# A SwiGLU feed-forward with seven-product duos: the last difference of the up product is written into its PSUM bank, and one plain weight tile waits for the duo's end

## The chip, the cores and the metric

The kernel runs on one core of a Trainium2 chip. The metric is the device time of one launch in microseconds (us). The engines are named as in the profile: PE (TensorE, matmuls), PEld (its weight loads), DVE (VectorE), ACT (ScalarE), POOL (GpSimd) and SP (SyncE, which here issues the weight loads from HBM).

## The reference

Two layers over 256 tokens of width 2048, in float32: gated linear attention, then a SwiGLU feed-forward; then shared keys and values, differential attention over them, and a second SwiGLU feed-forward. The change is in the feed-forward:

```python
def swiglu(h, w_gate_up, w_down):
    gate, up = jnp.split(h @ w_gate_up, 2, axis=-1)
    return (jax.nn.silu(gate) * up) @ w_down
...
        f = swiglu(rmsnorm(x, pre_ffn_g[i]), ffn_w_gate_up[i], ffn_w_down[i])
        x = x + rmsnorm(f, post_ffn_g[i])
```

`w_gate_up` is 2048 x 11264 and `w_down` 5632 x 2048.

## The kernel before

**Tiles.** Tokens are two blocks of 128. Weights are read once, in tiles of 128 x 1024 float32: two neighbouring 128-row pieces of the contraction, 512 columns each. SP loads a tile into one of five `raw` buffers; ACT casts it to a high part `hi` (L298); DVE subtracts to get the low part `lo` (L301). High and low parts lie in nine slots until PE is done with them. Each product of a 128 x 128 activation piece with a 128 x 512 weight piece takes three matmuls (high by high, high by low, low by high): `triple` (L484 to 488) in the duos, `mm_act` (L402 to 413) elsewhere.

**Duos.** The 5632 gate columns are 11 chunks of 512, the up columns 11 more. Chunk 0 is multiplied plainly. Each of chunks 1 to 10 is a duo: gate chunk c and up chunk 11 + c together, for both token blocks, over eight steps s of the contraction. A plain step costs eight products (24 matmuls, two weight tiles: w1 of the gate, w2 of the up). A fast step (0, 2, 3, 4, 5, 6; for chunk 1 only 0, 2, 4, 6) takes seven products (21 matmuls) on sums and differences, in Strassen's manner. Its weight tiles are called a, b, c and d: DVE forms the sums in place (four operations at L333), a, b and c are converted as tiles of 1024 columns, d as one of 512. The prepared activation sums are `f_ffn_fast` and `f_ffn_rest`; `h_ffn` holds the plain activations.

**Banks.** The products of a duo go to eight PSUM banks called `ps[0]` to `ps[7]`: 0 to 5 from a pool of six (`acc` in the profile), 6 and 7 from a pool of two (`tp`), which the transposes use as well. When the last fast step is done, `early` combines banks 0, 4, 5 and 6. Plain steps add the gate's products to banks 1 and 3 (one per token block), the up's to 2 and 7; when the last plain step has finished a bank, `late` adds it to what `early` left. For the gate, ACT then takes the Silu (L1208); for the up part, `gated` (L1190) multiplies it by the gate. The result `sg` is transposed on PE (L655) for the down product (`gate_T`).

**Order.** The tile framework puts each engine's work in an order of its own from the order in which it is issued. `weight_stream` fixes the order of the weight tiles and so of SP's loads. `take` converts ahead as far as the buffers allow. `behind(n)` issues its work behind the conversion of the nth tile ahead, so its number says how many conversions stand before an operation in DVE's queue; `urgent` lets an operation go to the front of what is ready; `defer(n, ...)` issues work n ticks of the matmul loops later. Between duos, the down product adds to banks that ACT has filled from `f_ffn` (L464) and that ACT copies back (L1261).

Of the kernel before, what the change touches and what calls it, by code (L numbers as in the profile page):

```python
# [15 lines left out]
ALU = mybir.AluOpType  # L16
AX = mybir.AxisListType

P = 128
D = 2048  # L20
SEQ = 256
KT = D // P
C = 512
# [21 lines left out]
SKEW, LAST_SKEW = 7, 8  # L45
CHAIN = (3, 4, 5, 6)
FIRST_X = {1: [(1, 0), (0, 1)], 3: [(1, 1)], 5: [(0, 2)], 7: [(1, 2)], 9: [(0, 3)], 11: [(1, 3)]}
NRAW, NRING = 5, 9
EARLY_BEHIND, LATE_BEHIND, DOWN_BEHIND, GATE_BEHIND = 3, 3, 0, 0
NEW_SUMS = ('w_g',)  # L50
V_BEGIN, V_EVERY, V_Q = 16, 3, 1

# [1 line left out]
def ffn_pairs(c):  # L54

    return FAST_SECOND if c == 1 else FAST_FFN
# [26 lines left out]
def weight_stream():  # L83

    out = []

    def chunk(name, n, ns=8, s0=0):
        out.extend((name, (n, s0 + s), "plain") for s in range(ns))

    def block(name, n):  # L90
        out.extend((name, (n, s), "plain") for s in range(2))

    def duo(c1, c2, fast):
        for s in range(8):
            if s in fast:
                out.extend(("duo", (c1, c2, s), kind) for kind in ("a", "b", "c", "d"))
            else:
                out.extend((name, (n, s), "plain") for name, n in (c1, c2))

    def ffn(i):  # L100
        for kind, which, *chunks in ffn_steps():
            if kind == "down":
                out.extend((f"w_d{i}", (c, 2 * which[0] + s), "plain") for c, s in down_order(which, *chunks))
            elif which == 0:
                chunk(f"w_gu{i}", 0)
                chunk(f"w_gu{i}", 11)
# [12 lines left out]

    def middle_duo(name, fast):  # L120
        chunk(name, 0)
        duo((name, 1), (name, 2), fast)
        chunk(name, 3)

    middle_duo("gla_w_out", FAST_OUT)
    ffn(0)
    chunk("w_v", 0)
    chunk("w_v", 3)
    duo(("w_v", 1), ("w_v", 2), FAST_V)
    for name in ("w_k", "diff_w_q"):  # L130
        for n in range(KT):
            block(name, n)
    middle_duo("diff_w_out", FAST_OUT)
    ffn(1)
    return out

# [52 lines left out]
class Trunk:  # L189
# [142 lines left out]
    def add(self, out, in0, in1):  # L332
        return self.nc.vector.tensor_tensor(out=out, in0=in0, in1=in1, op=ALU.add)  # L333
# [145 lines left out]
            for u in range(n, len(order)):  # L479
                run(u, b)  # L480

    def triple(self, ps, a, w, j, first, last):
        nc = self.nc
        ah, al = a  # L484
        wh, wl = (t[:, j * C : (j + 1) * C] for t in w)
        nc.tensor.matmul(ps, ah, wh, start=first, stop=False)  # L486
        nc.tensor.matmul(ps, ah, wl, start=False, stop=False)  # L487
        nc.tensor.matmul(ps, al, wh, start=False, stop=last)  # L488

    def duo_act(self, aT, forms, fast, c1, c2, early, late):  # L490

# [688 lines left out]
    def gated_duo(self, hT, forms, w, c, rs, new_sg):  # L1180

        nc = self.nc
        made = []

        def op(out, in0, in1, how):
            nc.vector.tensor_tensor(out=out, in0=in0, in1=in1, op=how)

        def gated(b, up):
            sg = made[0]
            nc.vector.scalar_tensor_tensor(  # L1190
                out=sg[:, b, :], in0=up, scalar=rs[b], in1=sg[:, b, :], op0=ALU.mult, op1=ALU.mult
            )

        def early(ps):
            made.extend((new_sg(), self.scratch(), self.scratch()))
            sg, v, y = made
            nc.scalar.copy(sg[:, 0, :], ps[0])
            op(v, ps[5], sg[:, 0, :], ALU.subtract)
            op(sg[:, 1, :], ps[6], v, ALU.subtract)
            op(y, ps[4], sg[:, 1, :], ALU.subtract)  # L1200
            op(v, ps[4], v, ALU.add)

        def late(bank, ps):
            sg, v, y = made
            if bank in (1, 3):
                b = bank // 2
                op(sg[:, b, :], ps[bank], sg[:, b, :], ALU.add)
                nc.scalar.activation(sg[:, b, :], sg[:, b, :], AF.Silu, scale=rs[b])  # L1208
            else:
                b, part = (0, v) if bank == 2 else (1, y)  # L1210
                op(part, ps[bank], part, ALU.add)
                gated(b, part)

        self.duo_apart(hT, forms, ffn_pairs(c), ((w, c), (w, 11 + c)), early, late)
        return made[0]

    def ffn(self, fp, hT, rs, gi, wgu, wd, post, after, name, reload, side=None):
        nc = self.nc
        self.narrow, self.n_narrow = (fp, 2, 2), 0
        forms = Forms(FAST_FFN, range(8), self.whole(4, [P, 4, 2, 4, P], f"{name}_fast", F32R))  # L1220
# [7 lines left out]
        first, last = FF_GROUPS[0], FF_GROUPS[-1]  # L1228
# [42 lines left out]
        f = []  # L1271
        plan = ffn_steps()
        for n, (kind, which, *chunks) in enumerate(plan):
            if kind == "up":
                sg = self.gated_duo(hT, forms, wgu, which, rs, new_sg) if which else gated_first()
                follow = plan[n + 1]
                wait = 4
                if follow[0] == "down" and which not in follow[1]:
                    wait = 2 * len(down_order(*follow[1:])) + 1
                self.defer(wait, lambda sg=sg, c=which: gate_T(sg, c))  # L1280
                continue
            chunks, skew = chunks[0], 0
            if not f:
                f.append(self.whole(5, [P, 2, D], name))
                if side:
                    self.defer(5, side)
            if which == last:
                if chunks[0] == 0:
                    reload()
                else:  # L1290
                    skew = LAST_SKEW
                for c in chunks:
                    gains[c] = self.gain(post, c)

# [158 lines left out]
    def run(self):  # L1453
        nc, tc, t = self.nc, self.tc, self.t
        self.setup()
        self.pool_lo.update((3, 5))
        hT = self.pair(0, "h_mix0")
        rs = []

        def reload(src, name):  # L1460
            self.x = self.whole(4, [P, 2, D], name)
            for b in range(2):
                nc.sync.dma_start(self.x[:, b, :], src[b])

        with tc.tile_pool(name="gla", bufs=1) as gp:
            oT = self.gla(gp, hT, rs)
            rs = []
            x_mix0 = self.dram.tile([2, P, D], F32, tag="x_mix0", name="x_mix0")
            hT = Split([])
# [179 lines left out]
```

## Time and profile before

| what | value |
|---|---|
| median of three runs | 2168.73 us (2167.71 to 2168.75) |
| profiled execution | 2168.14 us, its span 2166.4 us |
| PE busy in the span | 2151.2 us (99%) |
| DVE busy | 1953.3 us (90%) |
| ACT busy | 1374.2 us (63%) |
| the duos of the first feed-forward | about 430 to 1045 us of the span |
| the duos of the second | about 1510 to 2123 us of the span |

In the rows of the profile `acc<-lo,h_ffn` means output from inputs, with the buffers' numbers left out; "x4" counts instructions, and a bracket at the end says how long the engine had been idle before and what released it. A matmul's shown duration overlaps the next one's, so the distance between starts tells PE's speed. DVE's operations overlap a little in the same way.

### The profile page before, as it was taken

The numbers are of one execution on the slowest core, as the hardware profiler recorded it, in microseconds if no ns is written. First come the engines' busy times: TensorE is split into PE (matmuls) and PEld (weight loads), VectorE is DVE, ScalarE is ACT, GpSimd is POOL, SyncE is SP. The second block draws the span as 40 slices with busy tenths as digits, with TensorE's granted clock in tenths as the row PEclk, the third lists the DMA queues.
The fourth block names the chain that finished last, engine by engine and source line by source line (L and its number), as shares of the span: only waits on it lengthen the run. The fifth ranks groups of instructions, "written<-read, shape, count | busy, mean of one in ns | idle before, by whom it ended". The sixth has DMA issues, their size and how long they took to land.

```text
span 2166.4 us, 28415 instructions
## 1 busy us (share of the span) xinstructions
PE 2151.2 (99%) x10044; PEld 1787.7 (83%) x10044; DVE 1953.3 (90%) x2686; ACT 1374.2 (63%) x1926; POOL 37.1 (2%) x66
## 2 busy tenths in 40 slices
PE   9999999999999999999999999999999999999998
PEld 8888788888888888888778888888888888888886
DVE  7989988999999999999798567889999999999996
ACT  8756655666666666666776445556656666666664
POOL 1000000000000000000000000000000000000000
PEclk9999999999999999999999999999999999999999
DMA  8546566666565666656767655465665566665664
GB/s 310 166 150 192 174 226 219 219 199 227 173 209 203 211 211 195 223 190 211 254 200 245 185 179 159 155 226 202 225 195 187 177 207 214 212 209 201 203 225 155
DMA packets 123317, 440.10 MB, mean 203 GB/s; under 512 B 13900, under 2 KB 16629, under 8 KB 121381
## 3 DMA queue, kind: packets, MB, share of 16 engines
q1 hardware_dynamic: 121996, 436.44, 60.4%
q10 hardware_dynamic: 1176, 1.84, 0.2%
q8 instruction: 79, 1.29, 0.2%
q14 instruction: 66, 0.53, 0.1%
HBM read 429.82 MB, written 9.97 MB: 203 GB/s over the span
## 4 chain that ended last, share of the span: by engine, by line
PE 93%; DVE 4%; issue 1%; ACT 1%; DMA 1%; SPq 0%; POOL 0%; DVEq 0%; POOLq 0%; ACTq 0%
PE acc L488 12%; PE acc L487 12%; PE acc L486 12%; PE acc L413 11%; PE acc L412 11%; PE acc L411 11%; PE acc L634 8%; PE acc L635 4%; PE tp L487 2%; PE tp L486 2%; PE tp L488 2%; DVE lo L301 2%; PE tp L655 1%; DVE raw L333 1%; DMA raw<-in_w_d_dram 1%
## 5 line engine op out<-in xcount | busy, mean ns | idle before, releaser
L301 DVE TENSOR_TENSOR lo<-raw,hi 128x1024 fp32r<-128x1024 f32 x921 | 1096.2, 1220 | 115.1 <-ACT hi L298 108.8
L298 ACT CAST hi<-raw 128x1024 fp32r<-128x1024 f32 x923 | 943.9, 1051 | 356.5 <-DVE raw L333 91.5
L412 PE MATMUL acc<-lo,f_ffn_gT 128*128 128x512 f32 x704 | 273.5, 389 | 0.1
L411 PE MATMUL acc<-hi,f_ffn_gT 128*128 128x512 f32 x704 | 270.4, 389 | 0.0
L413 PE MATMUL acc<-hi,f_ffn_gT 128*128 128x512 f32 x704 | 269.0, 389 | 0.0
L487 PE MATMUL acc<-lo,h_ffn 128*128 128x512 f32 x612 | 238.7, 390 | 0.0
L488 PE MATMUL acc<-hi,h_ffn 128*128 128x512 f32 x612 | 238.4, 389 | 0.0
L486 PE MATMUL acc<-hi,h_ffn 128*128 128x512 f32 x612 | 227.8, 390 | 0.0
L333 DVE TENSOR_TENSOR raw<-raw 128x512 f32<-128x512 f32 x232 | 159.5, 687 | 3.4
L411 PEld LDWEIGHTS acc<-hi,f_ffn_gT 128*128 128x128 f32 x704 | 132.2, 188 | 28.4 <-issue 0.6
L412 PEld LDWEIGHTS acc<-lo,f_ffn_gT 128*128 128x128 f32 x704 | 132.1, 188 | 27.9 <-DVE lo L301 0.6
L413 PEld LDWEIGHTS acc<-hi,f_ffn_gT 128*128 128x128 f32 x704 | 132.2, 188 | 27.4
L486 PEld LDWEIGHTS acc<-hi,h_ffn 128*128 128x128 f32 x612 | 114.9, 188 | 24.2 <-ACT hi L298 0.4
L488 PEld LDWEIGHTS acc<-hi,h_ffn 128*128 128x128 f32 x612 | 114.9, 188 | 23.5
L487 PEld LDWEIGHTS acc<-lo,h_ffn 128*128 128x128 f32 x612 | 114.9, 188 | 23.5
L298 ACT CAST hi<-sum 128x512 fp32r<-128x512 f32 x72 | 44.8, 622 | 101.1 <-DVE sum L333 101.1
L634 PE MATMUL acc<-h_q,hi 128*128 128x512 f32 x256 | 92.5, 401 | 0.0
L634 PE MATMUL acc<-h_kv,hi 128*128 128x512 f32 x256 | 90.7, 399 | 0.0
L634 PE MATMUL acc<-h_mix,hi 128*128 128x512 f32 x256 | 90.6, 398 | 0.0
L1261 ACT COPY f_ffn<-acc 128x512 f32<-128x512 f32 x80 | 45.8, 586 | 66.4 <-PE acc L413 66.4
L298 ACT CAST f_ffn_rest<-sum 128x512 fp32r<-128x512 f32 x56 | 34.9, 623 | 80.9 <-DVE sum L333 80.9
L333 DVE TENSOR_TENSOR sum<-raw,raw 128x512 f32<-128x512 f32 x116 | 79.4, 685 | 0.0
(415 smaller groups left out, 4128.6 us busy)
## 6 DMA issues: line engine op xcount, KB each, us to landing
raw<-in_w_gu_dram SPq DMA_DIRECT2D x352, 512.0 KB, 4.5
raw<-in_w_d_dram SPq DMA_DIRECT2D x176, 512.0 KB, 4.8
raw<-in_gla_w_r_dram SPq DMA_DIRECT2D x32, 512.0 KB, 4.8
raw<-in_gla_w_v_dram SPq DMA_DIRECT2D x32, 512.0 KB, 4.1
raw<-in_gla_w_out_dram SPq DMA_DIRECT2D x32, 512.0 KB, 4.5
raw<-in_w_v_dram SPq DMA_DIRECT2D x32, 512.0 KB, 4.4
raw<-in_w_k_dram SPq DMA_DIRECT2D x32, 512.0 KB, 4.4
raw<-in_diff_w_q_dram SPq DMA_DIRECT2D x32, 512.0 KB, 3.5
```

The costliest lines, as they stand in the source:

```text
L298: cast = nc.scalar.copy(hi, src)
L301: rest = eng.tensor_tensor(out=lo, in0=src, in1=hi.bitcast(F32), op=ALU.subtract)
L333: return self.nc.vector.tensor_tensor(out=out, in0=in0, in1=in1, op=ALU.add)
L411: nc.tensor.matmul(ps, ah, rh, start=(kt == 0 and not onto), stop=False, skip_group_check=onto)
L412: nc.tensor.matmul(ps, ah, rl, start=False, stop=False, skip_group_check=onto)
L413: nc.tensor.matmul(ps, al, rh, start=False, stop=(kt == 2 * ns - 1), skip_group_check=onto)
L486: nc.tensor.matmul(ps, ah, wh, start=first, stop=False)
L487: nc.tensor.matmul(ps, ah, wl, start=False, stop=False)
L488: nc.tensor.matmul(ps, al, wh, start=False, stop=last)
L634: nc.tensor.matmul(ps, lh, aT.both(kt), start=(kt == 0), stop=False)
L635: nc.tensor.matmul(ps[:, SEQ:], ll, aT.hi(kt), start=False, stop=(kt == KT - 1))
L1261: nc.scalar.copy(fc, ps)
```

## The change

`gated_duo` uses a new function, `duo_seeded`, in place of `duo_apart`.

- `early` writes the difference that it used to keep in scratch `y` straight into bank 7, before any matmul of that bank. All matmuls of bank 7 then add onto it (none starts the bank afresh).
- `late` of bank 7 no longer adds bank and scratch; `gated` reads the bank itself.
- Where a step other than 7 is plain (step 1; for chunk 1 steps 1, 3 and 5), its w1 tile stays in place, and its w2 tile is held back to step 7: the stream there is kept w2, w1 of step 7, w2 of step 7. Kept w2 goes to bank 2 at once and to bank 7 after banks 1 and 3 are finished.
- Banks 2 and 6 now come from the pool `tp`; 0, 1, 3, 4, 5 and 7 from `acc`.
- `early` is issued urgent, and EARLY_BEHIND falls from 3 to 1. The gate transposes of chunk 0 are deferred by 1 tick instead of 4.
- `reload_by_parts` and its two constants are added and not called.

```diff
-EARLY_BEHIND, LATE_BEHIND, DOWN_BEHIND, GATE_BEHIND = 3, 3, 0, 0
+EARLY_BEHIND, LATE_BEHIND, DOWN_BEHIND, GATE_BEHIND = 1, 3, 0, 0
...
     def duo(c1, c2, fast):
+        apart = c1[0][:4] == "w_gu"
+        kept = [s for s in range(7) if s not in fast] if apart else []
         for s in range(8):
+            if s == 7:
+                out.extend((c2[0], (c2[1], s), "plain") for s in kept)
+            if s in kept:
+                out.append((c1[0], (c1[1], s), "plain"))
+                continue
...
+    def duo_seeded(self, aT, forms, fast, chunks, early, late):
...
+                ps[bank] = self.tp().rearrange("p j t -> p (j t)") if bank in (2, 6) else self.acc()
...
+            if last:
+                bank_of(7)
+                with self.behind(EARLY_BEHIND):
+                    self.urgent(early)(ps)
+        kept = [(s, self.take(w2, (n2, s))) for s in held]
+        for s, wp in kept:
+            plain(2, s, 0, wp, False)
+        wp = self.take(w1, (n1, 7))
+        for b, bank in enumerate((1, 3)):
+            plain(bank, 7, b, wp, True)
+        for s, wp2 in kept:
+            plain(7, s, 1, wp2, False, True)
+            self.free()
+        self.free()
+        wp = self.take(w2, (n2, 7))
+        plain(2, 7, 0, wp, True)
+        plain(7, 7, 1, wp, True, True)
+        self.free()
...
-            made.extend((new_sg(), self.scratch(), self.scratch()))
-            sg, v, y = made
+            made.extend((new_sg(), self.scratch()))
+            sg, v = made
...
-            op(y, ps[4], sg[:, 1, :], ALU.subtract)
+            op(ps[7], ps[4], sg[:, 1, :], ALU.subtract)
...
-            else:
-                b, part = (0, v) if bank == 2 else (1, y)
-                op(part, ps[bank], part, ALU.add)
-                gated(b, part)
-
-        self.duo_apart(hT, forms, ffn_pairs(c), ((w, c), (w, 11 + c)), early, late)
+            elif bank == 2:
+                op(v, ps[bank], v, ALU.add)
+                gated(0, v)
+            else:
+                gated(1, ps[bank])
+
+        self.duo_seeded(hT, forms, ffn_pairs(c), ((w, c), (w, 11 + c)), early, late)
...
-                wait = 4
+                wait = 4 if which else 1
```

The order of work changes in the duos of both feed-forward stages. DVE at the end of chunk 5's duo in the first stage, before. `hs` and `sg` are the scratch and the gate buffer, `lo` rows are conversions, and the first L1186 row reads `ps[5]`:

```order
L301 TENSOR_TENSOR lo_1233_6434<-raw_1214_6347,hi_1232_6433 128x1024
L301 TENSOR_TENSOR lo_1236_6446<-raw_1205_6297,hi_1235_6445 128x1024
L301 TENSOR_TENSOR lo_1239_6463<-raw_1217_6359,hi_1238_6462 128x1024
L301 TENSOR_TENSOR lo_1242_6475<-raw_1225_6393,hi_1241_6474 128x1024
L301 TENSOR_TENSOR lo_1245_6487<-raw_1228_6405,hi_1244_6486 128x1024
L1186 TENSOR_TENSOR hs_1266_6559<-acc_1196_6270,sg_1265_6558 128x512
L301 TENSOR_TENSOR lo_1248_6499<-raw_1234_6437,hi_1247_6498 128x1024
L1186 TENSOR_TENSOR sg_1265_6558<-tp_1192_6258,hs_1266_6559 128x512
```

The same place on DVE now. `lo_1231` is the held-back tile, `lo_1234` the gate's tile of step 7, and `acc_1257` is bank 7:

```order
L309 TENSOR_TENSOR lo_1225_6407<-raw_1206_6320,hi_1224_6406 128x1024
L309 TENSOR_TENSOR lo_1228_6419<-raw_1197_6279,hi_1227_6418 128x1024
L309 TENSOR_TENSOR lo_1231_6436<-raw_1209_6332,hi_1230_6435 128x1024
L1259 TENSOR_TENSOR hs_1259_6533<-acc_1193_6267,sg_1258_6532 128x512
L309 TENSOR_TENSOR lo_1234_6448<-raw_1217_6366,hi_1233_6447 128x1024
L1259 TENSOR_TENSOR sg_1258_6532<-tp_1187_6248,hs_1259_6533 128x512
L309 TENSOR_TENSOR lo_1237_6460<-raw_1220_6378,hi_1236_6459 128x1024
L309 TENSOR_TENSOR lo_1240_6472<-raw_1226_6410,hi_1239_6471 128x1024
L1259 TENSOR_TENSOR acc_1257_6531<-acc_1198_6281,sg_1258_6532 128x512
```

Between tiles b and c of the last fast step (the first two rows of both pieces) and the first early operation there stood three conversions, and now there is one, the held-back tile's. The write into bank 7 stands two conversions behind the gate's tile of step 7.

PE at the same place now, from the last matmul of bank 5 (`acc_1193`) to the first that needs `lo_1234`; `tp_1188` is bank 2, `acc_1182` and `acc_1194` are banks 1 and 3:

```order
L561 MATMUL acc_1193_6267<-hi_1227_6418,f_ffn0_rest_3649 128x512
L560 MATMUL acc_1194_6271<-lo_1228_6419,h_ffn0_1_3491 128x512
L561 MATMUL acc_1194_6271<-hi_1227_6418,h_ffn0_1_3491 128x512
L559 MATMUL acc_1182_6225<-hi_1233_6447,h_ffn0_1_3491 128x512
L559 MATMUL acc_1194_6271<-hi_1233_6447,h_ffn0_1_3491 128x512
L560 MATMUL tp_1188_6252<-lo_1231_6436,h_ffn0_0_3490 128x512
L561 MATMUL tp_1188_6252<-hi_1230_6435,h_ffn0_0_3490 128x512
L559 MATMUL tp_1188_6252<-hi_1230_6435,h_ffn0_0_3490 128x512
L560 MATMUL tp_1188_6252<-lo_1231_6436,h_ffn0_0_3490 128x512
L561 MATMUL tp_1188_6252<-hi_1230_6435,h_ffn0_0_3490 128x512
L559 MATMUL tp_1188_6252<-hi_1236_6459,h_ffn0_1_3491 128x512
L560 MATMUL acc_1182_6225<-lo_1234_6448,h_ffn0_1_3491 128x512
```

Eleven matmuls lie between the start of bank 5's last one and the first that takes `lo_1234`.

DVE at the end of chunk 10's duo in the first stage, before (`rs_ffn` rows are the gating products, whose result the transposes take):

```order
L1186 TENSOR_TENSOR hs_1838_9257<-tp_1777_9016,hs_1838_9257 128x512
L1186 TENSOR_TENSOR hs_1837_9256<-acc_1764_8959,hs_1837_9256 128x512
L301 TENSOR_TENSOR lo_1831_9241<-raw_1817_9187,hi_1830_9240 128x1024
L301 TENSOR_TENSOR lo_1834_9250<-raw_1820_9199,hi_1833_9249 128x1024
L301 TENSOR_TENSOR lo_1840_9278<-raw_1823_9208,hi_1839_9277 128x1024
L1190 SCALAR_TENSOR_TENSOR sg_1836_9255<-hs_1838_9257,rs_ffn0_1_3849,sg_1836_9255 128x512
L1190 SCALAR_TENSOR_TENSOR sg_1836_9255<-hs_1837_9256,rs_ffn0_0_3744,sg_1836_9255 128x512
```

And now (`acc_1823` is bank 7):

```order
L1259 TENSOR_TENSOR hs_1825_9220<-tp_1754_8939,hs_1825_9220 128x512
L309 TENSOR_TENSOR lo_1815_9192<-raw_1801_9138,hi_1814_9191 128x1024
L309 TENSOR_TENSOR lo_1818_9204<-raw_1804_9150,hi_1817_9203 128x1024
L1263 SCALAR_TENSOR_TENSOR sg_1824_9219<-hs_1825_9220,rs_ffn0_0_3744,sg_1824_9219 128x512
L1263 SCALAR_TENSOR_TENSOR sg_1824_9219<-acc_1823_9218,rs_ffn0_1_3849,sg_1824_9219 128x512
```

One add and one conversion fewer stand ahead of the gating products. On PE, the transposes of that gate stand 28 matmuls behind the last matmul of bank 7 in both stages.

More of the change, by code (lines that the diff above doesn't have):

```diff
@@ L47 @@
 FIRST_X = {1: [(1, 0), (0, 1)], 3: [(1, 1)], 5: [(0, 2)], 7: [(1, 2)], 9: [(0, 3)], 11: [(1, 3)]}
+RELOAD_BEGIN, RELOAD_EVERY = 4, 3
 NRAW, NRING = 5, 9
-EARLY_BEHIND, LATE_BEHIND, DOWN_BEHIND, GATE_BEHIND = 3, 3, 0, 0
+EARLY_BEHIND, LATE_BEHIND, DOWN_BEHIND, GATE_BEHIND = 1, 3, 0, 0
 NEW_SUMS = ('w_g',)
@@ L480, in down_act, with bank_of, add, plain @@
                 run(u, b)
-    def triple(self, ps, a, w, j, first, last):
+    def duo_seeded(self, aT, forms, fast, chunks, early, late):
+        ps, held = {}, []
+        (w1, n1), (w2, n2) = chunks
+        def bank_of(bank):
+            if bank not in ps:
+                ps[bank] = self.tp().rearrange("p j t -> p (j t)") if bank in (2, 6) else self.acc()
+                return True
+            return False
+        def add(bank, a, wp, j, last, onto=False):
+            first = bank_of(bank)
+            self.triple(ps[bank], a, wp, j, first and not onto, last, onto)
+        def plain(bank, s, b, wp, last, onto=False):
+            for j in range(2):
+                add(bank, aT.tokens(2 * s + j, b), wp, j, last and j == 1, onto)
+            if last:
+                with self.behind(LATE_BEHIND):
+                    late(bank, ps)
+            self.tick()
+        for s in range(7):
+            k1, k2 = 2 * s, 2 * s + 1
+            if s not in fast:
+                wp = self.take(w1, (n1, s))
+                for b, bank in enumerate((1, 3)):
+                    plain(bank, s, b, wp, False)
+                self.free()
+                held.append(s)
+                continue
+            f, last = forms.pairs.index(s), s == fast[-1]
+            plan = {
+                "a": ((0, aT.tokens(k1, 0)), (1, aT.tokens(k2, 0))),
+                "b": ((6, forms.fast(f, 2)), (2, forms.fast(f, 3))),
+                "c": ((5, forms.fast(f, 1)), (3, aT.tokens(k2, 1))),
+                "d": ((4, forms.fast(f, 0)),),
+            }
+            for kind, prods in plan.items():
+                wp = self.take("duo", (*chunks, s), kind)
+                for j, (bank, a) in enumerate(prods):
+                    add(bank, a, wp, j, last and bank in (0, 4, 5, 6))
+                self.free()
+                if kind != "d":
+                    self.tick()
+            if last:
+                bank_of(7)
[5 more added lines that the diff above has]
+        wp = self.take(w1, (n1, 7))
+        for b, bank in enumerate((1, 3)):
+            plain(bank, 7, b, wp, True)
+        for s, wp2 in kept:
+            plain(7, s, 1, wp2, False, True)
+            self.free()
+        self.free()
+        wp = self.take(w2, (n2, 7))
+        plain(2, 7, 0, wp, True)
+        plain(7, 7, 1, wp, True, True)
+        self.free()
@@ L483, in triple @@
+    def triple(self, ps, a, w, j, first, last, onto=False):
         nc = self.nc
@@ L485, in triple @@
         wh, wl = (t[:, j * C : (j + 1) * C] for t in w)
-        nc.tensor.matmul(ps, ah, wh, start=first, stop=False)
-        nc.tensor.matmul(ps, ah, wl, start=False, stop=False)
-        nc.tensor.matmul(ps, al, wh, start=False, stop=last)
+        nc.tensor.matmul(ps, ah, wh, start=first, stop=False, skip_group_check=onto)
+        nc.tensor.matmul(ps, ah, wl, start=False, stop=False, skip_group_check=onto)
+        nc.tensor.matmul(ps, al, wh, start=False, stop=last, skip_group_check=onto)
     def duo_act(self, aT, forms, fast, c1, c2, early, late):
@@ L1199, in early @@
             op(sg[:, 1, :], ps[6], v, ALU.subtract)
-            op(y, ps[4], sg[:, 1, :], ALU.subtract)
+            op(ps[7], ps[4], sg[:, 1, :], ALU.subtract)
             op(v, ps[4], v, ALU.add)
         def late(bank, ps):
-            sg, v, y = made
+            sg, v = made
             if bank in (1, 3):
@@ L1463, in reload, with reload_by_parts @@
                 nc.sync.dma_start(self.x[:, b, :], src[b])
+        def reload_by_parts(src, name):
+            self.x = x = self.whole(4, [P, 2, D], name)
+            for n in range(8):
+                b, c = n // 4, slice(n % 4 * C, (n % 4 + 1) * C)
+                self.defer(RELOAD_BEGIN + RELOAD_EVERY * n, lambda b=b, c=c: nc.sync.dma_start(x[:, b, c], src[b][:, c]))
         with tc.tile_pool(name="gla", bufs=1) as gp:
```

## The prediction

> **What bounds the kernel now.** I read the busy shares and the chain of the page first, then the windows over the two feed-forward stages, where the duos are.
>
> ```profile
> PE 2151.2 (99%) x10044; PEld 1787.7 (83%) x10044; DVE 1953.3 (90%) x2686; ACT 1374.2 (63%) x1926; POOL 37.1 (2%) x66
> PE 93%; DVE 4%; issue 1%; ACT 1%; DMA 1%; SPq 0%; POOL 0%; DVEq 0%; POOLq 0%; ACTq 0%
> ```
> ```profile
> core 0: us, PE busy (x) PEld busy (x) DVE busy (x) ACT busy (x) POOL busy (x), PEclk, DMA share, GB/s
> 450.00:980.00 530.00, 529.99 (x2371) 438.81 (x2370) 510.29 (x613) 344.30 (x414) 0.00 (x0) 1.00 0.62 207
> 980.00:1060.00 80.00, 78.94 (x355) 64.92 (x354) 73.79 (x86) 53.88 (x68) 0.00 (x0) 1.00 0.71 247
> 1560.00:2060.00 500.00, 500.00 (x2240) 414.84 (x2239) 482.16 (x574) 324.54 (x392) 0.00 (x0) 1.00 0.60 200
> 2060.00:2166.00 106.00, 97.50 (x436) 79.77 (x434) 83.81 (x106) 58.94 (x83) 1.10 (x2) 0.97 0.54 190
> ```
>
> In both long windows PE is busy all the time (529.99 of 530, 500.00 of 500) and DVE nearly so (96%). Only the windows at the two ends of the stages show PE idle. Since a matmul's end is modelled, I checked with starts: back to back, in a fast step, they stand 0.227 apart (717.15 to 717.38 below). I call that the step of PE.
>
> So PE is the bound, with DVE just behind it. The change adds and removes no matmul. It can therefore gain only what PE waits for in these stages, and lose wherever DVE's reserve is used up. The list of PE's waits has one entry in each feed-forward stage, for the last gate transposes (chunk 10):
>
> ```profile
> PE tp L655 <- DVE sg L1190: 1.0, 1, 1.0
> PE tp L655 <- DVE sg L1190: 0.3, 1, 0.3
> ```
> ```profile
> 1044.67 0.61 PE L411 MATMUL acc<-hi,f_ffn_gT 128*128 128x512 f32 x2
> 1046.30 1.09 PE L655 MATMUL tp<-ident,sg 128*128 128x128 f32 x8 [1.01 <-DVE sg L1190]
> 2123.14 0.61 PE L411 MATMUL acc<-hi,f_ffn_gT 128*128 128x512 f32 x2
> 2124.06 1.09 PE L655 MATMUL tp<-ident,sg 128*128 128x128 f32 x8 [0.31 <-DVE sg L1190]
> ...
> 1044.83 1.41 DVE L1190 SCALAR_TENSOR_TENSOR sg<-hs,rs_ffn,sg 128x512 f32<-128x512 f32 x2
> 1046.16 4.70 DVE L301 TENSOR_TENSOR lo<-raw,hi 128x1024 fp32r<-128x1024 f32 x4
> ```
>
> Two matmuls from 1044.67 leave PE ready at 1045.12; it starts the transposes at 1046.30, 0.06 after DVE's two gating products end (1046.24). That costs 1.18 us. At the second place PE is ready at 2123.59 and starts at 2124.06: 0.47. **The whole prize that I can see is 1.65 us.**
>
> How far DVE is behind in a fast step, and what it does at the end of a duo (chunk 5 of the first stage):
>
> ```profile
> 704.15 0.68 DVE L333 TENSOR_TENSOR sum<-raw,raw 128x512 f32<-128x512 f32 x1
> ...
> 710.84 0.69 DVE L333 TENSOR_TENSOR sum<-raw,raw 128x512 f32<-128x512 f32 x1
> ...
> 715.26 2.36 DVE L301 TENSOR_TENSOR lo<-raw,hi 128x1024 fp32r<-128x1024 f32 x2
> ...
> 719.81 0.68 DVE L1186 TENSOR_TENSOR hs<-acc,sg 128x512 f32<-128x512 f32 x1
> 720.41 1.22 DVE L301 TENSOR_TENSOR lo<-raw,hi 128x1024 fp32r<-128x1024 f32 x1
> ```
> ```profile
> 717.15 0.39 PE L487 MATMUL acc<-lo,f_ffn_rest 128*128 128x512 f32 x1
> 717.38 0.39 PE L488 MATMUL acc<-hi,f_ffn_rest 128*128 128x512 f32 x1
> ```
>
> The same sum comes back 6.69 us later (704.15 to 710.84), while PE needs 21 x 0.227 = 4.76 for that step: DVE loses 1.93 per fast step. A plain weight tile costs DVE (2.36 - 1.22) = 1.14 and gives PE 12 matmuls, 2.72: DVE gains 1.58. At the last fast step the conversion begun at 715.26 ends at 716.48, and PE takes it at 717.15: 0.67 us in hand. DVE's order of work at this place is what the change touches.
>
> **The change, part by part.**
>
> *The product's add that goes.* Durations by kind:
>
> ```profile
> L1186 DVE TENSOR_TENSOR hs<-acc,sg x40: 680/684/692, 467.3 to 2113.9; 128x512 f32<-128x512 f32 x40
> L1248 DVE SCALAR_TENSOR_TENSOR sg<-acc,rs_ffn,sg x4: 742/743/744, 431.8 to 1513.0; 128x512 f32<-128x512 f32 x4
> L1190 DVE SCALAR_TENSOR_TENSOR sg<-hs,rs_ffn,sg x40: 739/746/751, 479.9 to 2123.3; 128x512 f32<-128x512 f32 x40
> L464 ACT COPY acc<-f_ffn x80: 571/579/593, 594.9 to 2139.4; 128x512 f32<-128x512 f32 x80
> L1261 ACT COPY f_ffn<-acc 128x512 f32<-128x512 f32 x80 | 45.8, 586 | 66.4 <-PE acc L413 66.4
> ```
>
> One such operation occupies DVE for 0.60 (719.81 to 720.41; its 0.68 overlaps the next). Twenty duos: 12.0 us of DVE time, all of it beside a busy PE, so zero on the path.
>
> *The difference written into bank 7, the gate read from there.* Reading a bank instead of scratch costs the gating product nothing (743 ns against 746). No DVE write to a bank is in the trace. On ACT, a copy into a bank takes 579 ns against 586 out of one, so I take zero. Bounds: from 0.01 cheaper to, at worst, one more whole operation (0.60), which would merely undo the removal. It is off PE's path unless the seed is late: between the last matmul of bank 5 and the first of bank 7 the new order has 40 matmuls, 9.1 us (some 60 in three of the duos). In that stretch DVE has three narrow operations and three tile conversions, 3 x 0.60 + 3 x 1.14 = 5.2, after a start of 0.50 (below): over 3 us to spare, cost 0. The second gating product now waits for bank 7's last matmul; behind it in DVE's queue stand conversions that PE needs more than 5 us later.
>
> *The held-back tile.* One weight tile per duo (three for chunk 1) moves to the end: its load on SP's queue, its cast on ACT, its conversion on DVE and 12 matmuls.
>
> ```profile
> raw<-in_w_gu_dram SPq DMA_DIRECT2D x352, 512.0 KB, 4.5
> ```
>
> Number and sizes of loads stay; the load moves past those of the fast steps, which each come one place earlier. The DMA share is 0.62, so cost 0. On DVE the reserve at the end of the fast steps should fall by the 1.58 that the tile gave. But the previous duo's end, which now holds its own kept tile, gives the same 1.58 ahead of this duo, plus the 0.60 that is gone. I walked DVE's new list for chunk 5 from the evacuation on ACT that it stands behind at 683.20:
>
> ```profile
> 683.20 0.59 ACT L1261 COPY f_ffn<-acc 128x512 f32<-128x512 f32 x1 [0.77 <-PE acc L413]
> ```
>
> About 1.6 later (that copy, a cast of 1.05) DVE begins a conversion at 684.8. Up to the conversion in question come two tiles (2.3), seven narrow operations (4.3), three fast steps (3 x 6.69) and one tile (1.28 behind a narrow operation), and it takes 1.22 itself: its end is at 714.0. PE wants it 12 matmuls earlier than now, at 714.43: 0.45 in hand instead of 0.67. Cost 0; were these 0.45 used up, each further microsecond would cost PE one in every duo like this one.
>
> *The early operations moved forward: a new wait.* They now stand after one conversion of the end instead of three, so DVE comes to the first (which reads bank 5) before PE has finished that bank, and waits. Behind it in DVE's queue stands the low part of the gate tile for step 7, and PE waits for that. Twice the trace shows DVE waiting just so:
>
> ```profile
> 466.83 0.39 PE L488 MATMUL acc<-hi,f_ffn_rest 128*128 128x512 f32 x1
> 467.26 0.69 DVE L1186 TENSOR_TENSOR hs<-acc,sg 128x512 f32<-128x512 f32 x1 [1.15 <-PE acc L488]
> ...
> 1609.56 0.39 PE L488 MATMUL acc<-hi,f_ffn_rest 128*128 128x512 f32 x1
> 1610.06 0.69 DVE L1186 TENSOR_TENSOR hs<-acc,sg 128x512 f32<-128x512 f32 x1 [1.32 <-PE acc L488]
> 464.89 1.22 DVE L301 TENSOR_TENSOR lo<-raw,hi 128x1024 fp32r<-128x1024 f32 x1 [0.59 <-ACT hi L298]
> ```
>
> From the start of the bank's last matmul it takes 0.43 to 0.50 until DVE starts, then 0.61 to the conversion, 1.22 for it, and 0.06 until PE may go (above): 2.32 to 2.39. In the new order PE has 11 matmuls between, 2.49. **So 0.10 to 0.17 us are in hand, in 17 of the 20 duos** (chunk 1 of either stage and chunk 2 of the first have over 2 us). I take zero cost. The upper end is a conversion that waits another 0.59 for ACT's cast, as at 464.89: 0.59 - 0.14 = 0.45 per duo, 17 x 0.45 = 7.7 us. The lower end is 0.
>
> *Gate transposes.* Chunk 10's now stand 28 matmuls, 6.3 us, behind bank 7's last matmul; DVE needs after it at most 0.50, two conversions (2.3) and two gating products (1.41): 4.2. So both waits should go: -1.65. Chunk 0's, asked for sooner, stand behind more than 20 matmuls: 0.
>
> **The sum.** -1.65, of which I take 1.5, since a little may stay in front of the matmul after the transposes. The profiled execution took 2168.14 (span 2166.4 and 1.7 around it), 0.6 below the median 2168.73. From the median: **2167.2**. Changes under 0.2% (4.3 us) I count as no change, which is about what a measurement of this kernel can tell.
>
> **The rivals.**
>
> *The conversion behind the early operation is late (slower).* The place is the new wait above. For: only 0.10 to 0.17 in hand, repeated in 17 duos, and only 0.45 in hand just ahead of it. Against: both sides of that chain are rows of this trace. Each 0.1 beyond the reserve is 1.7 us; it decides from (1.5 + 4.3) / 17 = 0.34 beyond, so a conversion 0.5 late. At the upper end 2167.2 + 7.7 = 2174.9.
>
> *The removed time was on the path (faster).* If every microsecond taken from DVE came back: 2168.7 - 12.0 = 2156.7. The other reading of the page that speaks for it is PE's weight loads, busy 83%:
>
> ```profile
> L411 PEld LDWEIGHTS acc<-hi,f_ffn_gT 128*128 128x128 f32 x704 | 132.2, 188 | 28.4 <-issue 0.6
> ```
>
> Against: one load of 0.188 in every step of 0.227 is 83%, so this figure is what back-to-back matmuls give, and the list of waits has nothing else. The Trainium skill's "Perfetto Trace Analysis", section "Identifying the Most-Contended Engine", says that matmul occupancy is a poor measure and the share of weight-load time a better one; by that rule PE would have 17% to give and this rival would hold. The trace disagrees here: the steps between starts are even, with no room in them.
>
> *The waits at chunk 10 stay (no change).* If the transposes come as late to PE's order as before, nothing moves: 2168.7. For: the gating products stay last in the duo. Against: the 2 us counted above.
>
> *The seed is late.* It needs over 3 us more than counted, then costs 20 us for each further one; nothing in the trace is that slow.
>
> **How the numbers follow.** As forecast, 2164.5 to 2168.2: 0.58. Waits stay or small stalls eat the gain, 2168.2 to 2173.0: 0.23. Late conversion or seed, above 2173.0: 0.14. The removed time or part of it on the path, below 2164.4: 0.05. Leaving 0.05 below and about 0.12 above gives 2164.5 to 2174.0. The signs: faster 0.05, same 0.81, slower 0.14.
>
> **What would show it.** Right: PE busy for all of the long windows still; DVE's busy time about 12 us less over the kernel; no wait of the transposes for the gate; about 17 short waits of DVE for PE, near 0.6 each, before the first early operation; 180 narrow operations of the kind where there were 200. Wrong: PE waiting for a low part at the gate tile of step 7, duo after duo, or for the seed at bank 7; or a step between matmuls under 0.227, which would mean that PE had room all along.

## The result and the profile after

| | before | after |
|---|---|---|
| median of six runs | 2167.61 us (2166.94 to 2168.75) | 2176.32 us (2174.78 to 2177.02) |
| profiled execution | 2168.14 us | 2177.02 us |
| span of it | 2166.4 us | 2175.3 us |

The ratio after to before is 1.0039 (95% interval 1.0026 to 1.0052). The change makes the kernel 8.7 us slower, 9.1 us above the forecast of 2167.2 and 2.3 us above the upper end of the range.

The busy shares on the page of after, and the windows over the first three of the prediction's stretches of the feed-forward stages:

```profile
PE 2153.7 (99%) x10044; PEld 1785.1 (82%) x10044; DVE 1943.2 (89%) x2666; ACT 1376.0 (63%) x1926; POOL 38.4 (2%) x66
```
```profile
core 0: us, PE busy (x) PEld busy (x) DVE busy (x) ACT busy (x) POOL busy (x), PEclk, DMA share, GB/s
450.00:980.00 530.00, 527.81 (x2353) 434.62 (x2352) 504.70 (x603) 342.88 (x409) 0.00 (x0) 1.00 0.62 207
980.00:1060.00 80.00, 78.87 (x356) 64.84 (x355) 72.06 (x83) 54.81 (x70) 0.00 (x0) 1.00 0.71 245
1560.00:2060.00 500.00, 497.57 (x2219) 410.00 (x2218) 475.66 (x565) 320.31 (x384) 0.00 (x0) 1.00 0.59 199
```

DVE has 10.1 us less to do (1943.2 instead of 1953.3), and PE, which was busy through all of the two long windows, now stands idle in both: 18 and 21 fewer matmuls begin there (2353 instead of 2371, 2219 instead of 2240). The list of waits names what PE waits for, with the total in us, the number of times and the longest. Of after, for PE, two entries out of these stages:

```profile
PE acc L419 <- ACT acc L472: 5.5, 8, 1.2
PE acc L559 <- ACT hi L306: 1.3, 1, 1.3
```

L472 is the copy with which ACT fills a bank from `f_ffn` before the down product adds to it (L464 in before). It was never waited for in before. The end of chunk 5's duo in the first stage shows how that comes. After, ACT and then PE:

```profile
713.50 0.58 ACT L1270 COPY sg<-acc 128x512 f32<-128x512 f32 x1
713.98 2.00 ACT L306 CAST hi<-raw 128x1024 fp32r<-128x1024 f32 x2
716.28 1.05 ACT L306 CAST hi<-raw 128x1024 fp32r<-128x1024 f32 x1 [0.31 <-DMA raw<-in_w_d_dram]
718.74 1.05 ACT L306 CAST hi<-raw 128x1024 fp32r<-128x1024 f32 x1 [1.40 <-DMA raw<-in_w_d_dram]
719.69 1.10 ACT L472 COPY acc<-f_ffn 128x512 f32<-128x512 f32 x2
...
719.36 0.39 PE L561 MATMUL acc<-hi,h_ffn 128*128 128x512 f32 x1
720.33 0.50 PE L419 MATMUL acc<-hi,f_ffn_gT 128*128 128x512 f32 x1 [0.58 <-ACT acc L472]
720.66 0.39 PE L560 MATMUL tp<-lo,h_ffn 128*128 128x512 f32 x1
```

Before, the same place:

```profile
717.98 0.57 ACT L1197 COPY sg<-acc 128x512 f32<-128x512 f32 x1
718.83 1.05 ACT L298 CAST hi<-raw 128x1024 fp32r<-128x1024 f32 x1 [0.27 <-DMA raw<-in_w_d_dram]
719.78 0.58 ACT L464 COPY acc<-f_ffn 128x512 f32<-128x512 f32 x1
720.97 1.05 ACT L298 CAST hi<-raw 128x1024 fp32r<-128x1024 f32 x1 [0.61 <-DMA raw<-in_w_d_dram]
721.93 0.58 ACT L464 COPY acc<-f_ffn 128x512 f32<-128x512 f32 x1
...
723.27 0.39 PE L411 MATMUL acc<-hi,f_ffn_gT 128*128 128x512 f32 x1
```

Two things moved. In ACT's queue the two copies stood 2nd and 4th behind the copy of bank 0 (the first row, which is part of `early`); now they stand 5th and 6th, behind four casts, and the last of these waits 1.40 for a weight tile. On PE the first down matmul stood 26 matmuls behind bank 5's last one, and now stands 21 behind. Before, the copy ended at 720.36 and PE came at 723.27: 2.9 us to spare. Now PE would be ready at 719.36 + 0.23 = 719.59 and starts at 720.33, 0.06 after the copy: 0.74 lost. The next matmul follows 0.335 later instead of 0.227, another 0.11.

The weight tile itself is hardly later than before. Counted from bank 5's last matmul (717.38 before, 714.79 after), the cast of the second down tile starts at 3.59 before and at 3.95 after. What moved is the copy: it stood ahead of this cast and now stands behind it.

Measured so, from start to start less one step of 0.227, PE has 14 waits in the two feed-forward stages of after, 9.28 us: ten for these copies (7.19), two in chunk 10 for casts of gate or up weights that land late (1.63), two for low parts (0.46). Less the 1.65 of the transposes, which is gone, and with 14 x 0.11 for the slow second matmuls, that makes 9.2. The two profiled executions differ by 2177.02 - 2168.14 = 8.88.

### The profile page after: what moved, and what is told of

Its sections match the earlier page's. It is cut to its first block, busy times and chain, and to the rows that moved or that the text cites. A ratio compares the mean times of both kernels' runs of the same rounds, so it can differ in the third digit from the quotient of the medians.

```text
span 2175.3 us, 28407 instructions
## 1 busy us (share of the span) xinstructions
PE 2153.7 (99%) x10044; PEld 1785.1 (82%) x10044; DVE 1943.2 (89%) x2666; ACT 1376.0 (63%) x1926; POOL 38.4 (2%) x66
## 4 chain that ended last, share of the span: by engine, by line
PE 89%; DVE 5%; DMA 3%; ACT 2%; issue 1%; SPq 0%; POOL 0%; DVEq 0%; ACTq 0%; POOLq 0%
PE acc L419 11%; PE acc L421 11%; PE acc L420 11%; PE acc L559 10%; PE acc L560 10%; PE acc L561 10%; PE acc L707 8%; PE acc L708 4%; PE tp L560 3%; PE tp L561 3%; PE tp L559 3%; DVE lo L309 2%; DMA raw<-in_w_d_dram 2%; ACT hi L306 2%; DVE raw L341 1%
## 5 line engine op out<-in xcount | busy, mean ns | idle before, releaser
L341 DVE TENSOR_TENSOR raw<-sum,raw 128x512 f32<-128x512 f32 x116 | 79.3, 684 | 0.0
```

## The experiments

**The theories.** Theory 1: PE loses its time to ACT's copies for the next down chunk, which the new order puts behind casts of weights that are not there yet. Its rivals: the held-back tile makes weights late at the duo's end, and the copies are only where that shows (theory 2); the seed costs, by the write into the bank or by the bank being held longer (theory 3); the earlier place of the early operations costs time on DVE's side (the prediction's first rival); or DVE's removed time, or an equal time added, is itself on the path. Each kernel ran 4 to 11 times, beside before, whose medians were 2167.78 (the first four below), 2168.06 (the next four) and 2168.1 (the last three).

**e1: the copies issued ahead.** After, with the copies for the next down chunk issued inside `early`:

```diff
+    def banks(self, c, base):
+        ps = [self.acc(), self.acc()]
+        if base:
+            for i in range(2):
+                self.nc.scalar.copy(ps[i], base(c, i))
+        return ps
...
-                ps[c] = [self.acc(), self.acc()]
-                if base:
-                    for i in range(2):
-                        self.nc.scalar.copy(ps[c][i], base(c, i))
+                ps[c] = self.ahead.pop(c, None) or self.banks(c, base)
...
             op(sg[:, 1, :], ps[6], v, ALU.subtract)
+            if self.coming:
+                nxt, base = self.coming
+                self.ahead[nxt] = self.banks(nxt, base)
             op(ps[7], ps[4], sg[:, 1, :], ALU.subtract)
...
+                self.coming = (follow[2][0], part) if follow[0] == "down" and follow[1] != first else None
```

> The changed kernel, with ACT's two copies that fill the next down chunk's banks issued inside the early operations, so that on ACT they stand 1 and 4 places behind the copy of bank 0 instead of 5 and 6; everything else as in the change. Theory 1 (PE waits for these copies, which stand behind casts whose weight tile lands late; ten such waits, 7.2 us in the changed kernel's trace): they go, 2168.5 to 2170. Theory 2 (weights land late at the duo's end because of the held-back tile; the copies are only where it surfaces): the wait moves to the next cast or conversion, 2174 or more. Theory 3 (the seed itself costs: the write into the bank or the bank held longer): 2174 to 2176.

Measured: 2167.38, ratio 0.9999 (0.999 to 1.0008). The whole loss is gone. ACT and PE at chunk 5's end in e1, then its waits of PE in these stages:

```profile
713.49 0.58 ACT L1275 COPY sg<-acc 128x512 f32<-128x512 f32 x1
713.97 0.59 ACT L467 COPY acc<-f_ffn 128x512 f32<-128x512 f32 x1
...
716.39 0.58 ACT L467 COPY acc<-f_ffn 128x512 f32<-128x512 f32 x1
...
718.87 1.05 ACT L307 CAST hi<-raw 128x1024 fp32r<-128x1024 f32 x1 [0.91 <-DMA raw<-in_w_d_dram]
719.57 0.62 PE L420 MATMUL acc<-hi,f_ffn_gT 128*128 128x512 f32 x2
```
```profile
PE acc L420 <- ACT hi L307: 0.7, 1, 0.7
...
PE acc L565 <- DVE lo L310: 0.5, 1, 0.5
```

The copies now stand 1st and 4th behind the copy of bank 0; the weight tile is late all the same (0.91 at 718.87), but no copy stands behind it, and PE begins the down product at 719.57 with no wait. What is left are short waits in chunk 10, which take the place of the transposes' 1.65. The seed and the held-back tile are still there, so neither costs the time by itself. The time lies 1 us below the range expected of theory 1. The edit also made the planner (the part of the tile framework that orders each engine's work) put bank 7's first matmul 28 matmuls behind bank 5's last one instead of 40, so it isn't the copies alone that moved.

**e2: no copies at all.** After, with nothing to fill the banks with, so that the sums of earlier groups are left out:

```diff
-            base = None if which == first else part
+            base = None
```

> The changed kernel without ACT's copies into the down product's banks (the sums of the earlier groups are left out of the down product). Theory 1: PE's waits for the copies are gone, and 76 copies less on ACT let the casts run sooner: 2167 to 2169. Theory 2: the casts still wait for late weights, PE waits for conversions instead: 2173 or more. Theory 3: 2174 to 2176.

Measured: 2165.49, ratio 0.9989 (0.998 to 0.9998): 10.8 below after. Without the copies (80 of them, by ACT's count of 1846 instead of 1926) the rest of the change costs nothing. The 2 us below e1 are no gain in chunk 10: there PE waits 0.85 and 1.56 in e2, as much as the 0.90, 0.56 and 0.70 of e1. By the two profiled executions the difference lies outside the feed-forward stages: PE's wait of 1.0 for `h_kv` after the first stage is gone, and the 480 matmuls from about 1194 us on, on `h_kv` and `h_q`, take 83.0 us instead of 84.6, in another order. That part of the gain says nothing of the copies.

**e3: held-back tile and early order, but no seed.** After, with the difference kept in scratch and added at the end, as before the change:

```diff
-            op(ps[7], ps[4], sg[:, 1, :], ALU.subtract)
+            op(y, ps[4], sg[:, 1, :], ALU.subtract)
...
-                gated(1, ps[bank])
+                op(y, ps[bank], y, ALU.add)
+                gated(1, y)
```

> The changed kernel's order of weights (the up tile held back to the duo's end) and its early operations after one conversion, but no seed: the difference goes to scratch and is added to bank 7 at the end, as before. On ACT the copies stand 3 and 6 places behind the copy of bank 0, on PE the first is needed 27 matmuls after bank 5's last instead of 21. Theory 1: the copies are in time by about 1.5 us, so 2167 to 2169. Theory 2 (held-back tile): 2173 to 2177. Theory 3 (the seed): as before, 2167 to 2168.

Measured: 2174.63, ratio 1.0032 (1.0019 to 1.0044). The expectation from the first theory missed. The copies are not waited for here (they stand 3rd and 6th, the first of them with 3.9 to 4.7 us to spare in these duos), but something else is. PE's waits, and one of them with ACT's row:

```profile
PE acc L558 <- ACT hi L306: 4.5, 7, 1.2
```
```profile
1732.15 0.51 PE L558 MATMUL acc<-hi,f_ffn_rest 128*128 128x512 f32 x1 [0.55 <-ACT hi L306]
1731.05 2.00 ACT L306 CAST hi<-raw 128x1024 fp32r<-128x1024 f32 x2 [0.69 <-DVE raw L341]
```

At the last fast step of chunks 4, 6 and 8 of both stages PE waits for a cast, which waits for the sum that DVE forms late: DVE's reserve has run out. Six such places of 0.92 and one wait of 1.37 in chunk 10 make 6.9. The 1.65 of the transposes, which is gone here too, and the slow second matmuls nearly cancel, so that this is about the loss of 6.85. So the order with the held-back tile has a cost of its own, on DVE, and the add that the seed saves may be what pays for it. The next kernel shows whether that is so.

**e8: e3 without the add.** The scratch difference is still formed, but not added; the gate reads the bank, so the second token block's up product lacks it:

```diff
-                op(y, ps[bank], y, ALU.add)
-                gated(1, y)
+                gated(1, ps[bank])
```

> The held-back order without seed (the experiment that took 2174.6), with the add of bank 7 left out, so VectorE has the change's number of operations; the difference stays in scratch and is not added. Theory 4 (with the tile held back, VectorE's reserve at the end of the fast steps is used up in the even duos, and the 0.6 per duo decide): the twelve waits of PE for casts there, 5.5 us in that trace, go: 2167.5 to 2170. Rival (the held-back order itself is late, whatever VectorE's load): 2173 to 2175.

Measured: 2167.78, ratio 0.9999 (0.9991 to 1.0008). The waits of e3 are down to one:

```profile
PE acc L558 <- ACT hi L306: 0.9, 1, 0.9
```

In the held-back order 0.60 of DVE per duo decides over 6.9 us, and not the order alone. In the order of before it decides over less, as the next two show.

**e6 and e7: before, with one more operation per duo, and with the add left out.** e6 adds an operation of 0.60 beside the removed add; e7 leaves the add out, with the order of before:

```diff
                 op(part, ps[bank], part, ALU.add)
+                if bank == 7:
+                    op(v, part, part, ALU.add)
```
```diff
-                op(part, ps[bank], part, ALU.add)
-                gated(b, part)
+                if bank == 2:
+                    op(part, ps[bank], part, ALU.add)
+                    gated(b, part)
+                else:
+                    gated(b, ps[bank])
```

> The kernel before with one more 512-wide VectorE operation per duo, just ahead of the second gating product (it writes a scratch that is not read again). If VectorE's time in the duos is on the path, as the rival of the prediction has it, 20 x 0.6 = 12 us more: about 2180. If it lies beside PE with a reserve of 0.67 us in the tightest duos: 2167.5 to 2171.

> The kernel before with the one VectorE add per duo taken away that the change takes away, and nothing else: the difference is not added to bank 7, and the gate reads the bank alone. If the removed VectorE time is hidden beside PE: 2166.5 to 2168. If it was on the path: 2155 to 2160.

Measured: e6 2171.43, ratio 1.0014 (1.0005 to 1.0023); e7 2166.99, ratio 0.9996 (0.9987 to 1.0005). The busy shares of e6 and of e7:

```profile
PE 2152.6 (99%) x10044; PEld 1787.0 (82%) x10044; DVE 1963.3 (90%) x2706; ACT 1374.5 (63%) x1926; POOL 38.1 (2%) x66
```
```profile
PE 2150.8 (99%) x10044; PEld 1787.0 (82%) x10044; DVE 1941.2 (90%) x2666; ACT 1372.6 (63%) x1926; POOL 37.0 (2%) x66
```

Twelve us taken from DVE (12.1 by its busy time) bring nothing that can be measured; as many operations added (10.0 by busy time) cost 3.4. In e7 both waits of the transposes are gone, but PE waits for casts of the transposed gate instead (0.81 at 488.93, 1.50 at 1051.09). PE is the bound, and DVE stands so close behind it that time added to DVE shows and time taken from it does not. e6's waits of PE in the two stages come to 4.4 us between starts (before 1.65), half of them around a gate of the second stage, 1938 to 1944.

**e4: the early operations later again.** After with one number changed:

```diff
-EARLY_BEHIND, LATE_BEHIND, DOWN_BEHIND, GATE_BEHIND = 1, 3, 0, 0
+EARLY_BEHIND, LATE_BEHIND, DOWN_BEHIND, GATE_BEHIND = 3, 3, 0, 0
```

> The changed kernel with the early operations issued behind three conversions as before (two more than in the change). On PE the first down matmul now stands 26 matmuls behind bank 5's last instead of 21, 1.1 us later; on ACT the copies stand where they stood. Theory 1: waits of 0.7 go, those of 1.3 shrink to 0.2: 2168.5 to 2170.5. Theory 2: unchanged, 2175 to 2177. Theory 3: the seed is still written, 2174 to 2177.

Measured: 2198.37, ratio 1.014 (1.0126 to 1.0154). A miss by 28 us. The list of PE's waits:

```profile
PE acc L419 <- ACT acc L472: 23.7, 16, 2.3
```

The copy of bank 0 is part of `early` and moved back too, and the copies for the down product still stand 5th and 6th behind it (4th and 5th in chunk 10). So each comes later still. This is the first theory's mechanism with three and a half times the loss, 30.6 us, part of it by a slower clock (last section). It shows that with the seed the early place of `early` helps: without it the loss is larger.

**e5: before, with early operations ahead.** The early place alone:

```diff
-EARLY_BEHIND, LATE_BEHIND, DOWN_BEHIND, GATE_BEHIND = 3, 3, 0, 0
+EARLY_BEHIND, LATE_BEHIND, DOWN_BEHIND, GATE_BEHIND = 1, 3, 0, 0
...
-                    early(ps)
+                    self.urgent(early)(ps)
```

> The kernel before, with one part of the change alone: the early operations issued urgent and behind one conversion. No seed, nothing held back. On PE the first down matmul now stands 16 matmuls behind bank 5's last instead of 26 (2.3 us sooner), on ACT the copy for its bank 3 places behind the copy of bank 0 instead of 2. Theory 1 (PE waits for the copies): the 2 to 4 us that the copies had in hand are gone, waits of 0 to 1 us in some 16 duos, 2168.5 to 2176. Rival (the loss needs the seed or the held-back tile): 2167 to 2168.5.

Measured: 2174.21, ratio 1.003 (1.0019 to 1.0042). The number is near what was expected, the mechanism is another one: the first copies have 1.1 to 4.1 us to spare, and PE waits for the casts of the transposed gate in chunk 10, 2 us in each stage, after which its clock falls (last section). Five waits of 0.31 for casts, in even chunks as in e3, come on top. The profiled execution, 2176.48, was the slowest of the six, so its trace may show more than the median lost. The two long waits:

```profile
PE acc L411 <- ACT f_ffn_gT L657: 4.0, 2, 2.1
```

**e9: the seed, with the tile left in its place.** After, with the stream order of before; the plain tile is multiplied into bank 2 at once and kept for bank 7 only:

```diff
-        kept = [s for s in range(7) if s not in fast] if apart else []
+        kept = []
...
-                held.append(s)
+                wp = self.take(w2, (n2, s))
+                plain(2, s, 0, wp, False)
+                held.append((s, wp))
```

> The changed kernel with the weights in the order of before: the plain up tile comes at its old step and is used for bank 2 there, and is kept in its slot until bank 7 is seeded. Seed and early operations as in the change. On ACT the copies stand 5 and 6 places behind the copy of bank 0, as in the change; on PE the first is needed 20 matmuls behind bank 5's last (21 in the change). Theory 1 (the copies' place on ACT, which comes with the seed and not with the held-back tile): PE waits for them in most duos, 2174 to 2178. Theory 2 (the held-back tile makes the loss): 2167 to 2169.

Measured: 2182.49, ratio 1.0067 (1.0054 to 1.0079). The direction was right, the size larger. PE's waits:

```profile
PE acc L419 <- ACT acc L472: 11.2, 14, 1.6
```

From start to start these are 13.4 us, and with 14 x 0.11 for the slow second matmuls and without the 1.65 of the transposes they give 13.3. The profiled execution (2180.96) took 12.8 more than that of before; by the medians the loss is 14.4. So the copies' wait comes without the held-back tile too, and more of it.

**e10: e9 with the copies ahead**, by the edit of e1.

> As the experiment before this one (seed, weights in the old order), with ACT's copies issued inside the early operations: 1 and 4 places behind the copy of bank 0, needed 15 and 21 matmuls behind bank 5's last. Theory 1: the waits go, 2167 to 2169.5. Rival (the slot held through the duo is what costs there): as without it, 2174 or more.

Measured: 2166.02, ratio 0.9991 (0.9982 to 1.0), 16.5 below e9. The windows of e10, with columns as above:

```profile
450.00:980.00 530.00, 530.00 (x2369) 438.48 (x2368) 507.74 (x605) 345.86 (x414) 0.00 (x0) 1.00 0.63 207
980.00:1060.00 80.00, 80.00 (x363) 66.44 (x362) 73.30 (x85) 55.78 (x72) 0.00 (x0) 1.00 0.73 253
1560.00:2060.00 500.00, 500.00 (x2239) 414.59 (x2238) 480.97 (x569) 327.58 (x395) 0.00 (x0) 1.00 0.61 202
```

PE is busy for all of them, the end of the first stage (980 to 1060) included. This is the lowest time of any kernel here that computes the whole: 2.1 us below before, about the 1.65 that the prediction saw as the whole prize, and too little to be told apart with certainty.

**e11: e1 with the reload in parts**, the unused function of the change, in both stages (the first is shown), to see whether the reload of the residual delays chunk 10's last weights:

```diff
-    lambda: reload(x_mix0, "x_ffn0")
+    lambda: reload_by_parts(x_mix0, "x_ffn0")
```

> The changed kernel with the copies issued inside the early operations (2167.4), and with the 2 MB reload of x at the end of each feed-forward stage split into eight loads of 256 KB spread over the steps (the changed file's unused function). In that kernel's trace 2.2 us of PE's waits are left in the stages, all in chunk 10, for casts of weight tiles that land behind the reload. If the reload delays them: these waits go, 2165 to 2166.5, just faster than before. If the weights are late for another reason: 2167 to 2168.

Measured: 2168.03, ratio 1.0 (0.9992 to 1.0009). The time expected if the reload delays the weights did not come, and waits in chunk 10 stay (0.77, 0.40 and 0.68 between starts). But the edit does less than it was meant to: in its trace the eight loads of the first stage are issued between 1016.62 and 1021.57 (in e1 the two at 1016.47), still all ahead of the down weights' loads from 1023.32 on. So this leaves open whether the reload delays those weights.

```profile
PE acc L420 <- ACT hi L307: 1.1, 2, 0.6
```

**What stays open.** With the seed the planner puts the first copy five places behind the copy of bank 0 (after, e4, e9; four in chunk 10); without it, with the same early operations, three (e3). The experiments show what that costs, not why it is decided so. Why those weight tiles come when they do stays open too: no kernel here had more `raw` buffers.

## Why the prediction was wrong, point by point

**The step that failed** is the sum over the moved operations ("The early operations moved forward ... I take zero cost"). It followed DVE and PE and asked what stands behind DVE's new wait. ACT's queue was left out, though `early` begins with a copy on ACT and the down product with two more. The prediction even quotes these copies (L464), but as the price of a write to a bank and not as work that PE waits for. Their reserve, 2.9 us at chunk 5 in the trace of before, was there to be read: the row of the copy and the row of the first L411 behind it. The missing term measured 7.19 us from start to start, some 8 with the slow second matmuls; casts in chunk 10 (1.63) are most of the rest. e1, e2 and e10, which take the copies or their lateness away, bring the time to between 2165.5 and 2167.4, around the forecast. That e1's 2167.38 stands next to the forecast is partly luck: the 1.65 that the forecast counted on is eaten there by 2.16 of waits in chunk 10, and e2's time holds a gain from elsewhere.

**The removed add: right.** Forecast 0 on the path; e7 gives 2166.99 beside 2168.06, within what can be told. DVE fell by 10.1 us, not 12.0. The write into the bank isn't the reason: e8, which writes scratch instead, shows 1943.8. With the order of before the full amount goes (e7, 1941.2), and e3 has 1.5 more than before with as many operations, so the rest went with the new order.

**The seed: right as an operation, not as a change of order.** In after the write at chunk 5 took as long as an operation between buffers (the row below: 0.69), and PE waited for no seed. But the late place of ACT's copies comes with it: e9 has the seed without the held-back tile and waits, e3 has the held-back tile without the seed and doesn't wait for them.

```profile
719.90 0.69 DVE L1259 TENSOR_TENSOR acc<-acc,sg 128x512 f32<-128x512 f32 x1
```

**The held-back tile: right for this change.** Chunk 5's conversion at the last fast step, forecast to end at 714.0 with 0.45 in hand, ended at 713.91, and PE took it at 714.57: 0.66 in hand. The even chunks, which were not walked, have more in hand in after (at chunk 6 this conversion ended at 776.41 and PE took it at 777.57, 1.16). Even so it is the even chunks that run dry in e3, with 0.60 more per duo, so chunk 5 alone could not have shown how near the limit was.

```profile
711.41 3.63 DVE L309 TENSOR_TENSOR lo<-raw,hi 128x1024 fp32r<-128x1024 f32 x3
...
715.29 0.69 DVE L1259 TENSOR_TENSOR hs<-acc,sg 128x512 f32<-128x512 f32 x1 [0.25 <-PE acc L561]
715.90 1.21 DVE L309 TENSOR_TENSOR lo<-raw,hi 128x1024 fp32r<-128x1024 f32 x1
...
714.57 0.39 PE L560 MATMUL acc<-lo,f_ffn_rest 128*128 128x512 f32 x1
714.79 0.39 PE L561 MATMUL acc<-hi,f_ffn_rest 128*128 128x512 f32 x1
717.29 0.40 PE L560 MATMUL acc<-lo,h_ffn 128*128 128x512 f32 x1
```

**The new wait of DVE: right almost to the hundredth.** In these rows bank 5's last matmul starts at 714.79, DVE at 715.29 (0.50, as forecast at most), the conversion ends at 717.11 and PE takes it at 717.29: 0.18 in hand, forecast 0.10 to 0.17. DVE's list has the wait in every duo, 20 times, mean 0.58:

```profile
DVE hs L1259 <- PE acc L561: 11.5, 20, 1.7
```

The first rival stood on this chain, and its time, 2174.9, is close to the result. But its mechanism is not what happened: just two of the 14 waits, 0.23 us each (chunks 4 and 8 of the second stage), are for that low part. A number that fits is no evidence for the mechanism that gave it.

**Gate transposes: right and worth nothing.** Both waits for the gate are gone, but PE then waits elsewhere in chunk 10: in the first stage 0.19 for a cast and 1.26 for a copy, in the second 1.44 for a cast. Both casts are of gate or up weights. So the window from 980 to 1060 is as idle as before (78.87 busy, before 78.94). Only e10 keeps the gain.

**The signs named beforehand:** the 180 narrow operations (the gating products counted in), DVE's short waits and the missing transposes' wait came, and most of DVE's 12 us; PE busy through the long windows did not, and what it waited for was not on the list of what might go wrong.

## What to carry to other kernels

When a change moves operations, follow every engine's queue at that place, the lightly loaded ones too: ACT was busy 63% of the time, and an in-order queue still put a copy of 0.58 us, whose inputs had long been there, behind a cast that waited for a transfer. For each operation that PE waits for, read the reserve (its end against PE's start) in the trace of before; a reserve of 3 us was lost here to 2.5 us of lateness on one side and 1.1 us of earliness on the other. If such an operation needs nothing late, issue it early by hand, as e1 and e10 do, rather than leave its place to what happens to be ready.

## What the runs showed of the hardware

A wait of PE of little over 2 us can cost more than itself. In e4 PE waits 2.04 (2.43 between starts) at 662.14, and soon after its matmuls, which stood 0.23 apart, stand 0.43 apart for about 3 us. The rows and the windows, whose eighth figure is the granted clock:

```profile
662.14 0.50 PE L419 MATMUL acc<-hi,f_ffn_gT 128*128 128x512 f32 x1 [2.04 <-ACT acc L472]
...
664.16 0.63 PE L420 MATMUL acc<-lo,f_ffn_gT 128*128 128x512 f32 x1
664.59 0.63 PE L421 MATMUL acc<-hi,f_ffn_gT 128*128 128x512 f32 x1
```
```profile
660.00:664.00 4.00, 1.96 (x8) 1.53 (x8) 4.00 (x6) 3.44 (x5) 0.00 (x0) 0.94 1.01 382
664.00:667.00 3.00, 3.00 (x8) 2.33 (x8) 3.00 (x5) 3.00 (x5) 0.00 (x0) 0.51 0.91 318
667.00:672.00 5.00, 5.00 (x23) 4.12 (x23) 4.50 (x5) 2.72 (x4) 0.00 (x0) 1.00 0.83 297
```

The same happens after the two waits of e5, where the granted clock is 0.57:

```profile
1051.00:1055.00 4.00, 4.00 (x12) 3.13 (x11) 3.12 (x4) 1.37 (x2) 0.00 (x0) 0.57 0.88 301
2133.00:2137.00 4.00, 4.00 (x13) 3.10 (x12) 3.00 (x4) 1.46 (x2) 0.00 (x0) 0.57 0.92 360
```

A fourth case is in e4 after a gap of 2.71 at 1756.12. Each costs 1.4 to 1.6 us more than the wait itself (six to eight matmuls 0.43 apart, each 0.2 late). Three other gaps of e4, of 2.35 to 2.63 between starts, brought no such fall, so the length alone does not decide it. The Trainium skill's "TensorE: Matmul & The Clock Gate", section "Part 1: The HAM clock gate (the "warmup" mystery)", says that the clock falls to half after an idle window of about 3.4 us and that this window runs freely. The about 3 us at half clock agree with such a window; the fall after gaps of 2.15 to 2.71 us does not agree with a window that must be idle throughout.

The other surprise is small: behind each of the 14 waits of PE in after's two stages, 0.335 to 0.341 us lie between the starts of the first matmul and the second, instead of 0.227. So each of these waits costs 0.11 more than its distance between starts shows. The list of waits gives less still: 0.58 at 720.33, where 0.74 was lost between starts and 0.85 in all.
